# A two-model float32 block on one core: weights of the second half split once, kept in DRAM as two parts

## The chip, the cores and the metric

One core of one Trainium2 chip runs the whole program. The metric is device time in microseconds (us), the median of several runs; the kernel before takes 2792.99 us (2792.43 to 2793.49 in 3 runs). Engines are named TensorE (PE; its weight load PEld), VectorE (DVE), ScalarE (ACT), GpSimd (POOL) and SyncE (SP), which issues most of the DMAs.

## The reference, cut to what matters

Two models are chained over 1024 tokens of width 1024. The first has two layers: a short convolution (layer 1) and dilated attention with 8 heads and three rates (layer 2). The second has one sparse attention layer, in which every query keeps its 256 best keys, and a gated feed-forward with a short convolution.

```
y = short_conv_mixer(h, conv_w_in, conv_w_out)          # w0i, w0o
y = dilated_mixer(h, dil_w_in, dil_w_out, cos, sin)     # w1i, w1v, w1o
...
c_q, c_kv, k_idx, w_idx = split(h @ w_in)               # w2i, w2k
q = (c_q @ w_uq).reshape(B, T, A_HEADS, A_HEAD_DIM)     # w2uq
q_idx = (c_q @ w_qi)                                    # w2q
score = where(key_pos <= q_pos, einsum(wb, relu(q_idx . k_idx)), -inf)
_, sel = lax.top_k(score, n_sel)                        # 256 of up to 1024 keys
return o @ w_o                                          # w2uk, w2uv, w2o
...
u, v = split(h @ w_in, 2); u = conv(u) + conv_b         # w3i, D_FF = 2816
return (gelu(u) * v) @ w_out                            # w3o
```

The comments give the names that the kernel uses for the weights. All is float32.

## The kernel before, in words

Every large product is done as three matmuls: a float32 operand is split into a high part (a copy rounded to the matmul's float32r form) and a low part (the rest), and high x high, high x low and low x high are summed in PSUM (`gemm`, `mm3`). Splitting a weight block of 128 x 1024 costs a ScalarE copy (L338) and a subtraction (L339), on GpSimd unless told otherwise. `weight` (L332 to L340) does this through a ring of three slots, each of a raw, a high and a low buffer of 1024 words:

```
raw, hi, lo = (wring[j][i] for j in range(3))
dma(v(raw.f), src)
A.activation(hi.r[:, :n], raw.f[:, :n], AF.Copy)
(lo_engine or G).tensor_sub(lo.r[:, :n], raw.f[:, :n], hi.f[:, :n])
```

The tokens are worked in two chunks of 512. Layer 1's input and layer 2's input projection use a weight block for both chunks at once (48 matmuls of 512 columns). From layer 2's out-projection on, the chunks are worked at different times, and each weight block is loaded and split again for the second chunk (24 matmuls per load).

The order of the program: layer 1 with its modulation vectors (to about 280 us), its out-projection (`outproj` with w0o, to about 560), layer 2's values, then its 8 heads (`block` and `attend`, to about 1320). A head has seven blocks of w1i, a rotation of queries and keys (`rotate`, L691 to L702, on ScalarE, VectorE and GpSimd), and `attend`, which exchanges small statistics through DRAM (L765 to L774). Then `finish_layer1` (w1o), `project` (w2i, w2k, w2q), `keys` (w2uk, w2uv), and the selection: `topk` finds the 256th best score by a binary search of 31 steps over the bits of a float. Each step counts (L1222 on VectorE for some blocks of queries, L1219 on ScalarE for others) and decides (L1228, L1231, L1242: on one or two numbers per partition, VectorE). The first search runs with `project` and `keys` of the first chunk; the second with the out-projection w2o of the first chunk and the start of its feed-forward. `attention` works the heads (w2uq is split in `head_query`, K and V are loaded on GpSimd's queue), `finish_dsa` is w2o, `ffn_in` is w3i (44 blocks per chunk), `ffn_out` w3o (24 blocks per chunk). The second chunk's attention is interleaved with the first chunk's `ffn_in`.

Each engine works its instructions in a fixed order that is written at build time by a scheduler with a timeline model; buffers of the arena (`ar.new`) are pages that are handed out in the program's order. SP's queue is one such order: a DMA that waits holds back all DMAs behind it.

## Time and profile before

| | |
|---|---|
| median of 3 runs | 2792.99 us |
| profiled execution: time, span | 2787.4 us, 2785.7 us |
| granted TensorE clock, mean (1.0 is 2.4 GHz) | 0.977 |
| TensorE busy | 2609.2 us (94%) |
| VectorE busy | 1588.0 us (57%) |
| ScalarE busy | 1196.7 us (43%) |
| GpSimd busy | 1333.1 us (48%) |
| moved by DMA | 345.18 MB, mean 124 GB/s |

Busy shares are means over stages with different limits, so the table only says that TensorE is the engine to look at. What a stage loses is TensorE's idle time in it, together with time that it spent at the lower clock; what ends that idle time stands in the waits of the stage.

### The profile page before, as it was taken

Reading aid. Unit: us, or ns where it says so; the run is one execution under the profiler, and the core shown is the slowest. Engines: PE = TensorE matmul, PEld = TensorE weight load, DVE = VectorE, ACT = ScalarE, POOL = GpSimd, SP = SyncE. Lnnn points to the kernel's source line nnn. Section 1 sums busy time; section 2 is a strip of 40 time slices with the busy share of each in tenths; the row PEclk is TensorE's granted clock in tenths of the full one; section 3 lists DMA queues with packets and bytes.
Section 4 is the critical chain, followed back from the end, with each engine's and each line's share of the span. In section 5 each row is a group of like instructions: output and inputs, shape, how many; then the busy total and the mean of one; then the engine's idle time right before and its main releaser. Section 6 shows DMA issues by size and latency. Waiting matters only on the chain. (4 is left out here: it accounts for less than half of the span.)

```text
span 2785.7 us, 33753 instructions
## 1 busy us (share of the span) xinstructions
PE 2609.2 (94%) x12070; PEld 2134.6 (77%) x12070; DVE 1588.0 (57%) x3188; ACT 1196.7 (43%) x2032; POOL 1333.1 (48%) x918
## 2 busy tenths in 40 slices
PE   8998999999999999999899778887999989999998
PEld 7876888788888888888777556766787868876787
DVE  7687223204565556556775998997766640434411
ACT  4211224324444544445435667665555543232322
POOL 1122337425645663565475564444544475444453
PEclk9999999999999999999999889999999999999999
DMA  7487224411111111111334534533444643443432
GB/s 289 163 269 242 82 76 165 149 50 56 59 45 64 61 48 52 61 61 55 122 126 151 190 98 141 198 116 113 147 140 134 220 149 106 146 145 133 146 116 72
DMA packets 159141, 345.18 MB, mean 124 GB/s; under 512 B 18386, under 2 KB 58362, under 8 KB 158972
## 3 DMA queue, kind: packets, MB, share of 16 engines
q1 hardware_dynamic: 149612, 317.71, 34.5%
q0 software_dynamic: 9216, 25.17, 3.1%
q8 instruction: 95, 1.56, 0.2%
q14 instruction: 74, 0.61, 0.1%
q10 hardware_dynamic: 144, 0.14, 0.0%
HBM read 285.67 MB, written 58.86 MB: 124 GB/s over the span
## 5 line engine op out<-in xcount | busy, mean ns | idle before, releaser
L254 PE MATMUL p<-page,wring 128*128 128x512 f32 (+2 forms) x8586 | 2022.0, 393 | 80.9 <-DVE page L1476 15.1
L254 PEld LDWEIGHTS p<-page,wring 128*128 128x128 f32 (+1 forms) x8586 | 1598.1, 189 | 440.4 <-POOL wring L339 24.7
L339 POOL TENSOR_TENSOR wring<-wring,wring 128x1024 fp32r<-128x1024 f32 (+1 forms) x283 | 687.8, 2431 | 761.4 <-ACT wring L338 668.3
L254 PE MATMUL p<-page,page 128*128 128x512 f32 (+5 forms) x2816 | 578.6, 350 | 57.4 <-ACT page L345 11.4
L254 PEld LDWEIGHTS p<-page,page 128*128 128x128 f32 (+1 forms) x2816 | 460.3, 196 | 147.4 <-ACT page L814 15.0
L338 ACT ACTIVATE wring<-wring 128x1024 fp32r<-128x1024 f32 (+1 forms) x283 | 293.8, 1040 | 404.4 <-PE p L254 373.1
L346 POOL TENSOR_TENSOR page<-page,page 128x512 fp32r<-128x512 f32 (+2 forms) x111 | 168.2, 1522 | 219.1 <-ACT page L345 209.8
L345 ACT ACTIVATE page<-page 128x512 fp32r<-128x512 f32 (+2 forms) x168 | 110.5, 667 | 306.6 <-DMA page<-d 164.0
L693 POOL TENSOR_TENSOR page<-page,page 128x512 f32<-128x512 f32 x96 | 131.0, 1373 | 128.2 <-ACT page L692 127.8
L299 DVE SCALAR_TENSOR_TENSOR page<-page,page 128x1024 f32<-128x1024 f32 x88 | 117.2, 1332 | 34.2 <-DMA page<-wmod 33.7
L695 DVE TENSOR_TENSOR page<-p,page 128x512 f32<-128x512 f32 x96 | 65.2, 685 | 121.1 <-ACT page L692 104.9
L1496 DVE SCALAR_TENSOR_TENSOR page<-p,page,page 128x512 f32<-128x512 f32 (+1 forms) x17 | 12.2, 719 | 204.2 <-PE p L254 204.2
L346 DVE TENSOR_TENSOR page<-page,page 128x512 fp32r<-128x512 f32 (+1 forms) x57 | 65.2, 1152 | 95.4 <-ACT page L345 90.1
L1469 DVE TENSOR_SCALAR page<-page,page 128x512 f32<-128x512 f32 x44 | 71.7, 1629 | 80.0 <-ACT page L1463 80.0
L702 POOL TENSOR_TENSOR page<-page,page 128x512 fp32r<-128x512 f32 x64 | 97.2, 1519 | 33.3 <-ACT page L701 33.3
L1219 ACT ACTIVATE page<-page,page 128x1024 bf16<-128x1024 f32 (+1 forms) x93 | 86.7, 932 | 60.3 <-DVE page L1242 47.1
L700 DVE TENSOR_TENSOR page<-page 128x512 f32<-128x512 f32 x64 | 82.3, 1295 | 50.0 <-POOL page L693 50.0
L691 ACT ACTIVATE page<-p 64x512 f32<-64x512 f32 x96 | 57.2, 596 | 93.0 <-PE p L254 63.5
L1475 ACT ACTIVATE page<-page 128x512 f32<-128x512 f32 x44 | 27.8, 631 | 141.5 <-DVE page L1473 141.4
L701 ACT ACTIVATE page<-page 128x512 fp32r<-128x512 f32 x64 | 57.0, 890 | 71.7 <-DVE page L700 71.3
L641 DVE SCALAR_TENSOR_TENSOR page<-p,page,page 128x512 f32<-128x512 f32 x48 | 35.8, 746 | 85.0 <-PE p L254 84.0
L1222 DVE TENSOR_SCALAR_CACHE_REDUCE page<-page,page 128x768 bf16<-128x768 f32 (+1 forms) x93 | 81.5, 876 | 1.5
(206 smaller groups left out, 2332.2 us busy)
## 6 DMA issues: line engine op xcount, KB each, us to landing
page<-wmod SPq DMA_DIRECT2D x88, 512.0 KB, 4.3
wring<-w3i SPq DMA_DIRECT2D x88, 512.0 KB, 3.4
d<-page SPq DMA_DIRECT2D x137, 256.0 KB, 2.3
page<-d SPq DMA_DIRECT2D x121, 256.0 KB, 3.2
wring<-w1i SPq DMA_DIRECT2D x56, 512.0 KB, 3.2
d<-page SPq DMA_DIRECT2D x32, 512.0 KB, 4.5
page<-d POOLq DMA_DIRECT2D x32, 512.0 KB, 6.8
wring<-w3o SPq DMA_DIRECT2D x32, 512.0 KB, 3.6
```

The costliest lines, as they stand in the source:

```text
L254: lastn["mm"] = T.matmul(out, lhsT=l, rhs=r, start=start, stop=stop)
L299: V.scalar_tensor_tensor(w.f, w.f, 1.0, sil[j // 6].f, op0=OP.mult, op1=OP.mult, accum_out=m)
L338: A.activation(hi.r[:, :n], raw.f[:, :n], AF.Copy)
L339: (lo_engine or G).tensor_sub(lo.r[:, :n], raw.f[:, :n], hi.f[:, :n])
L345: A.activation(hi.r[:, :n], src, AF.Copy)
L346: (engine or V).tensor_sub(lo.r[:, :n], src, hi.f[:, :n])
L693: G.tensor_mul(sw.f, sw.f, rope[1].f[:, CH(c)])
L700: V.tensor_tensor(a.f, a.f, sw.f, op=OP.add)
L702: G.tensor_sub(out[1], shape(a.f), out[2])
L1219: A.activation(junk.b[:, 0:sc.n], sc.f, AF.Sign, scale=-1.0, bias=at, accum_out=one)
L1222: V.tensor_scalar(junk.b[:, 0:sc.n], sc.f, at, None, op0=OP.is_ge, op1=OP.add, accum_out=one)
L1469: V.tensor_scalar(g.f[:, :512], tv(2), kc(2), col("fb")[:, f:f + 1], op0=OP.mult, op1=OP.add)
```

## The change

A generator `ready` goes over w1o, w2i, w2k, w2q, w2uk, w2uv, w2uq, w2o, w3i and w3o, 102 blocks. For each it loads the block, copies the high part on ScalarE, subtracts on VectorE, and writes both parts to a DRAM tensor. Its steps are taken in the out-projection of layer 1 and in layer 2's heads; what is left is finished behind the last head. `weight` of such a block is then one DMA of both parts (1 MB for a block of 128 x 1024), for either chunk. The ring keeps its nine buffers, as three pairs of high and low and three raw ones; behind layer 2 the raw ones become a fourth pair. `weight_own`, which split one block of w1o into buffers of its own, goes.

```diff
-        wring = []
-        for j in range(3):
-            t = views(sp.tile([128, 1024 * NRING], F32, name=f"wring{j}"))
-            wring.append([Buf(None, None, t, 1024 * i, 1024) for i in range(NRING)])
+        pair = lambda t, i: tuple(Buf(None, None, t, 2048 * i + 1024 * j, 1024) for j in range(2))
+        t = views(sp.tile([128, 2048 * NRING], F32, name="wring"))
+        wring = [pair(t, i) for i in range(NRING)]
+        pairs = [t[0][:, 2048 * i:2048 * i + 2048] for i in range(NRING)]
+        wraw = views(sp.tile([128, 1024 * NRING], F32, name="wraw", tag="wraw"))
+        wraw = [Buf(None, None, wraw, 1024 * i, 1024) for i in range(NRING)]
...
+        def ready(names):
+            for name in names:
+                if name == "w3o":
+                    srcs = {(k, a): I[name][k][:, a:a + m] for k in range(8)
+                            for a, m in ((0, 8), (8, 8), (16, 6))}
...
+                prepared[name] = {}
+                for i, src in srcs.items():
+                    n = math.prod(src.shape[1:])
+                    raw, hi = ar.new(n), ar.new(n)
...
+                    dma(flat, src)
+                    A.activation(hi.r[:, :n], raw.f[:, :n], AF.Copy)
+                    V.tensor_sub(raw.r[:, :n], raw.f[:, :n], hi.f[:, :n])
+                    t = dram([128, 2, n])
+                    dma(t[:, 0], hi.f[:, :n])
+                    dma(t[:, 1], raw.f[:, :n])
+                    prepared[name][i] = Ready(t)
+                    raw.free()
+                    hi.free()
+                    yield
...
         def weight(src, k=8, m=128, lo_engine=None):
-            i = wat[0] % NRING
+            i = wat[0] % len(wring)
...
-            raw, hi, lo = (wring[j][i] for j in range(3))
+            hi, lo = wring[i]
             v = lambda a: a[:, :n].rearrange("p (k m) -> p k m", k=k)
+            if isinstance(src, Ready):
+                dma(pairs[i].rearrange("p (l n) -> p l n", l=2)[:, :, :n], src.t)
+                return v(hi.r), v(lo.r)
+            raw = wraw[i]
...
+        later = Steps(ready(["w1o", "w2i", "w2k", "w2q", "w2uk", "w2uv", "w2uq", "w2o", "w3i", "w3o"]))
...
                     p = block(off + 8 * g + h)
+                    later.go()
...
             p = block(56 + h)
+            later.go(2)
...
             attend(h, q, k, vs, sz)
+            later.go(3)
+        later.finish()
...
+        t = views(sp.tile([128, 1024 * NRING], F32, name="wring2", tag="wraw"))
+        wring.append(pair(t, 0))
+        pairs.append(t[0][:, 0:2048])
...
-                p = gemm(weight(I["w2i"][b]), H2, (c,))[c]
+                p = gemm(weight(prepared["w2i"][b]), H2, (c,))[c]
...
-            raw, w = ar.new(296), new2(296)
-            dma(raw.f[:, 0:256], I["w2uq"][h])
-            split(*w, raw.f[:, 0:256], engine=G)
-            raw.free()
+            w = new2(296)
+            for i in range(2):
+                dma(w[i].f[:, 0:256], prepared["w2uq"][h].t[:, i])
...
-                w = weight(I["w3i"][f])
+                w = weight(prepared["w3i"][f])
```

The line `later.go()` also stands in `each` of layer 1's out-projection. The other uses (w1o, w2k, w2q, w2uk, w2uv, w2o, w3o) are changed like w2i. The lines of the changed kernel lie higher: the ring's subtraction stays in `weight`, L357, L359, L361 and L362 are the load, the subtraction and the two stores of `ready`, and L381 is the ring's load of raw blocks.

The scheduler writes the order of all engines anew. Three places follow, as the order of instructions on an engine; a row has the line, the operation, out<-in by buffer names, and the shape.

GpSimd in the out-projection of the first chunk's sparse attention, with the second search (L402 adds squares, L382 is a power). Before:

```order
L339 TENSOR_TENSOR wring_65<-wring_63,wring_64 128x1024 x3
L402 TENSOR_TENSOR page_11443<-page_11443,page_12721 128x512
L339 TENSOR_TENSOR wring_65<-wring_63,wring_64 128x1024
L402 TENSOR_TENSOR page_11443<-page_11443,page_12755 128x512
L339 TENSOR_TENSOR wring_65<-wring_63,wring_64 128x1024
L402 TENSOR_TENSOR page_11443<-page_11443,page_12789 128x512
L339 TENSOR_TENSOR wring_65<-wring_63,wring_64 128x1024
```

The change (L446 and L426 are the same adds and the power):

```order
L446 TENSOR_TENSOR page_11995<-page_11995,page_13258 128x512
L446 TENSOR_TENSOR page_11995<-page_11995,page_13290 128x512
L446 TENSOR_TENSOR page_11995<-page_11995,page_13322 128x512
L446 TENSOR_TENSOR page_11995<-page_11995,page_13354 128x512
L446 TENSOR_TENSOR page_11995<-page_11995,page_13386 128x512
L446 TENSOR_TENSOR page_11995<-page_11995,page_13418 128x512
L426 TENSOR_TENSOR page_3919<-page_3919,page_65 128x4
```

The weight subtractions between the adds are gone; so it is in all of GpSimd's order behind layer 2.

VectorE in a head of layer 2 (L695 and L698 are steps of the rotation, L346 a split of the values, L933 the gate). Before:

```order
L698 TENSOR_TENSOR page_7432<-page_6735 128x64x8
L346 TENSOR_TENSOR page_7841<-page_7498,page_7840 128x1024
L695 TENSOR_TENSOR page_7626<-p_7775,page_2578 128x512
L698 TENSOR_TENSOR page_7432<-page_7626 128x64x8
L933 SCALAR_TENSOR_TENSOR page_7626<-page_7626,p_7847 128x512
```

The change (L729, L732, L390 and L969 are the same steps):

```order
L359 TENSOR_TENSOR page_7847<-page_7847,page_7854 128x1024
L359 TENSOR_TENSOR page_7862<-page_7862,page_7025 128x1024
L732 TENSOR_TENSOR page_7018<-page_7855 128x64x8
L729 TENSOR_TENSOR page_7826<-p_8237,page_2592 128x512
L732 TENSOR_TENSOR page_7722<-page_7826 128x64x8
L729 TENSOR_TENSOR page_7847<-p_8238,page_2592 128x512
L732 TENSOR_TENSOR page_7722<-page_7847 128x64x8
L390 TENSOR_TENSOR page_8310<-page_7862,page_8309 128x1024
L359 TENSOR_TENSOR page_7847<-page_7847,page_7854 128x1024
L969 SCALAR_TENSOR_TENSOR page_7854<-page_7854,p_8316 128x512
```

Three of a head's nine or ten preparations now stand among these steps.

SP's queue in a head of layer 2 (L863 stores a head's result, L922 loads its values). Before:

```order
L337 DMA wring_63<-w1i 128x1024 x2
L863 DMA d_3151<-page_6648 128x512 x2
L337 DMA wring_63<-w1i 128x1024
L922 DMA page_6544<-d_3153 128x8x128
L337 DMA wring_63<-w1i 128x1024 x2
L922 DMA page_6735<-d_3153 128x1024
```

The change:

```order
L362 DMA d_6490<-page_5375 128x1024
L357 DMA page_6204<-w3i 128x1024
L362 DMA d_6271<-page_5367 128x1024
L357 DMA page_6168<-w3i 128x1024
L361 DMA d_6417<-page_6189 128x1024
L381 DMA wraw<-w1i 128x1024
L362 DMA d_6417<-page_6168 128x1024
L357 DMA page_6189<-w3i 128x1024
L381 DMA wraw<-w1i 128x1024
```

Loads and stores of the preparations now stand between the loads of w1i.

## Rows read from the trace of the kernel before

**Rows 1.** The page's first part: busy us (share of the span) xinstructions.
```profile
PE 2609.2 (94%) x12070; PEld 2134.6 (77%) x12070; DVE 1588.0 (57%) x3188; ACT 1196.7 (43%) x2032; POOL 1333.1 (48%) x918
```

**Rows 2.** Stretches: length, busy PE PEld DVE ACT POOL, clock, DMA share, GB/s.
```profile
696.40:1323.20 626.80, 618.04 (x3148) 520.53 (x3147) 375.90 (x803) 298.15 (x549) 350.14 (x260) 1.00 0.17 56
1323.20:1532.10 208.90, 193.09 (x898) 154.10 (x896) 139.86 (x226) 98.97 (x174) 121.73 (x72) 0.98 0.40 133
1532.10:1741.10 209.00, 161.57 (x722) 124.17 (x722) 195.64 (x581) 142.47 (x326) 112.96 (x130) 0.90 0.47 143
1741.10:1950.00 208.90, 174.69 (x720) 138.18 (x720) 189.36 (x415) 130.55 (x210) 94.68 (x54) 0.94 0.43 142
1950.00:2228.60 278.60, 267.64 (x1315) 222.32 (x1316) 181.18 (x410) 152.95 (x239) 132.24 (x118) 0.98 0.50 161
2228.60:2298.20 69.60, 59.06 (x241) 46.08 (x240) 31.76 (x30) 29.41 (x45) 52.16 (x31) 0.93 0.47 149
2298.20:2785.70 487.50, 465.73 (x2080) 379.65 (x2078) 141.00 (x165) 142.04 (x185) 229.65 (x114) 0.99 0.38 123
```

**Rows 3.** Timeline from 1754 us: start us, us, engine, line, operation, xcount.
```profile
1754.83 20.34 PE L254 MATMUL p<-page,wring 128*128 128x512 f32 x89
1754.90 0.16 DVE L1242 SCALAR_TENSOR_TENSOR page<-page 128x2 int32<-128x2 int32 x1
...
1756.35 4.77 POOL L339 TENSOR_TENSOR wring<-wring,wring 128x1024 fp32r<-128x1024 f32 x2 [9.89 <-ACT wring L338]
1756.50 2.27 DVE L1242 SCALAR_TENSOR_TENSOR page<-page 128x2 int32<-128x2 int32 x1
...
1765.00 0.16 DVE L1228 TENSOR_SCALAR page<-page 128x2 int32<-128x2 f32 x1
```

**Rows 4.** VectorE by form, 1532.1 to 1950.0 us: xcount | busy us, mean ns.
```profile
L1242 DVE SCALAR_TENSOR_TENSOR page<-page 128x2 int32<-128x2 int32 x60 | 23.8, 403 | 0.5
L1222 DVE TENSOR_SCALAR_CACHE_REDUCE page<-page,page 128x512 bf16<-128x512 f32 x31 | 23.1, 744 | 0.6
...
L1242 DVE SCALAR_TENSOR_TENSOR page<-page 128x1 int32<-128x1 int32 x59 | 19.5, 352 | 0.3
L1228 DVE TENSOR_SCALAR page<-page 128x2 int32<-128x2 f32 x32 | 16.9, 528 | 0.2
```

**Rows 5.** Groups of instructions of the whole span, columns as rows 4.
```profile
L339 POOL TENSOR_TENSOR wring<-wring,wring 128x1024 fp32r<-128x1024 f32 (+1 forms) x283 | 687.8, 2431 | 761.4 <-ACT wring L338 668.3
...
L338 ACT ACTIVATE wring<-wring 128x1024 fp32r<-128x1024 f32 (+1 forms) x283 | 293.8, 1040 | 404.4 <-PE p L254 373.1
```

**Rows 6.** Stretches of rows 2, the instructions of L339 alone.
```profile
1532.10:1741.10 209.00, 23.05 (x10) 0.90 0.47 143
1741.10:1950.00 208.90, 66.79 (x27) 0.94 0.43 142
```

**Rows 7.** TensorE's waits, 2228.6 to 2785.7 us: us in total, times, longest.
```profile
PE p L254 <- POOL wring L339: 9.9, 22, 1.7
PE p L254 <- ACT page L345: 4.4, 1, 4.4
PE p L254 <- DVE page L346: 2.6, 1, 2.6
```

**Rows 8.** Groups of instructions of the whole span, columns as rows 4.
```profile
L693 POOL TENSOR_TENSOR page<-page,page 128x512 f32<-128x512 f32 x96 | 131.0, 1373 | 128.2 <-ACT page L692 127.8
...
L510 DVE TENSOR_TENSOR page<-page,page 128x1024 fp32r<-128x1024 f32 x8 | 9.7, 1220 | 0.2 <-ACT page L509 0.2
```

**Rows 9.** Timeline of SP at the start, columns as rows 3.
```profile
13.27 0.33 SPq L298 DMA_DIRECT2D page<-wmod  x1
14.55 0.33 SPq L307 DMA_DIRECT2D page<-wshift  x1
```

**Rows 10.** Timeline of TensorE at the start, columns as rows 3.
```profile
42.25 32.99 PE L254 MATMUL p<-page,page 128*128 128x512 f32 x158 [0.65 <-DVE page L412]
```

**Rows 11.** DMA issues: out<-in, queue, xcount, KB each, median us to landing.
```profile
wring<-w3i SPq DMA_DIRECT2D x88, 512.0 KB, 3.4
```

More of the change, by code (lines that the diff above doesn't have):

```diff
@@ L328, in emit, with __init__ @@
         wat = [0]
+        class Ready:
+            def __init__(self, t):
+                self.t = t
+        def ready(names):
[3 more added lines that the diff above has]
+                            for a, m in ((0, 8), (8, 8), (16, 6))}
+                elif name in ("w2k", "w2q"):
+                    srcs = {0: I[name]}
+                else:
+                    srcs = {i: I[name][i] for i in range(I[name].shape[0])}
+                prepared[name] = {}
+                for i, src in srcs.items():
+                    n = math.prod(src.shape[1:])
+                    raw, hi = ar.new(n), ar.new(n)
+                    flat = raw.f[:, :n]
+                    if len(src.shape) == 3:
+                        flat = flat.rearrange("p (k m) -> p k m", k=src.shape[1])
+                    dma(flat, src)
[8 more added lines that the diff above has]
+                    yield
+        prepared = {}
         def weight(src, k=8, m=128, lo_engine=None):
-            i = wat[0] % NRING
+            i = wat[0] % len(wring)
             wat[0] += 1
             n = k * m
-            raw, hi, lo = (wring[j][i] for j in range(3))
+            hi, lo = wring[i]
             v = lambda a: a[:, :n].rearrange("p (k m) -> p k m", k=k)
+            if isinstance(src, Ready):
+                dma(pairs[i].rearrange("p (l n) -> p l n", l=2)[:, :, :n], src.t)
+                return v(hi.r), v(lo.r)
+            raw = wraw[i]
             dma(v(raw.f), src)
@@ L619, in emit, with outproj @@
                 modvec(pending.pop(0))
-        def weight_own(src, bufs):
-            raw, hi, lo = ar.new(1024), *new2(1024)
-            dma(raw.f.rearrange("p (k m) -> p k m", k=8), src)
-            A.activation(hi.r, raw.f, AF.Copy)
-            G.tensor_sub(lo.r, raw.f, hi.f)
-            raw.free()
-            bufs.extend((hi, lo))
-            return tuple(b.r.rearrange("p (k m) -> p k m", k=8) for b in (hi, lo))
-        def outproj(win, Y, c, gate, xold, xnew, each, apart=()):
-            for k in range(8):
-                mine = []
-                w = weight_own(win[k], mine) if k in apart else weight(win[k])
-                p = gemm(w, Y, (c,))[c]
-                for b in mine:
-                    b.free()
+        later = Steps(ready(["w1o", "w2i", "w2k", "w2q", "w2uk", "w2uv", "w2uq", "w2o", "w3i", "w3o"]))
+        def outproj(win, Y, c, gate, xold, xnew, each):
+            for k in range(8):
+                p = gemm(weight(win[k]), Y, (c,))[c]
                 lastn[3] = lastn["mm"]
@@ L908, in emit @@
                     p = block(off + 8 * g + h)
+                    later.go()
                     for c in range(2):
@@ L974, in each @@
                 xs.append(x)
-            for _ in outproj(I["w1o"], Yc, c, mods[:, 40:48], X1, None, each,
-                             () if c else (3,)):
+            for _ in outproj(prepared["w1o"], Yc, c, mods[:, 40:48], X1, None, each):
                 yield
@@ L1095, in project @@
             normed(0, col("gq"))
-            p = gemm(weight(I["w2k"], 8, 72), H2, (c,), 72)[c]
+            p = gemm(weight(prepared["w2k"][0], 8, 72), H2, (c,), 72)[c]
             kx = ar.new(512)
@@ L1115, in project @@
             free_h(H2, c)
-            whi, wlo = weight(I["w2q"], 2, 512)
+            whi, wlo = weight(prepared["w2q"][0], 2, 512)
             for b in range(4):
@@ L1139, in keys @@
             for i in range(2):
-                whi, wlo = weight(I["w2uk"][i])
+                whi, wlo = weight(prepared["w2uk"][i])
                 for h in range(4):
@@ L1149, in keys @@
             for i in range(2):
-                whi, wlo = weight(I["w2uv"][i], 2, 512)
+                whi, wlo = weight(prepared["w2uv"][i], 2, 512)
                 for t in range(4):
@@ L1434, in each @@
                 xs.append(x)
-            drive(outproj(I["w2o"], Y2, c, mods[:, 64:72], XF, X3, each))
+            drive(outproj(prepared["w2o"], Y2, c, mods[:, 64:72], XF, X3, each))
             free_h(Y2, c)
@@ L1522, in ffn_out @@
                     for a, n in parts:
-                        accumulate(p, weight(I["w3o"][k][:, a:a + n], n), a, n, whole)
+                        accumulate(p, weight(prepared["w3o"][k, a], n), a, n, whole)
                     finish(p, k, x, whole)
                 else:
-                    ws = [(weight(I["w3o"][k][:, a:a + n], n), a, n) for a, n in parts]
+                    ws = [(weight(prepared["w3o"][k, a], n), a, n) for a, n in parts]
                     for w in ws:
```

3 lines of the change are left out of this document (1 added, 2 removed).

## The prediction

> **What bounds the kernel now.** I read the page's busy times first, then the busy time of each engine by stretch, then the waits of the stretches in which TensorE stands still. TensorE is busy for 2609.2 of 2785.7 us [rows 1], so 176.5 us of idle time are all that any change around it can win, beside what the clock gives back. The stretches say where the 176.5 us lie [rows 2]. Layer 2's heads lose 626.80 - 618.04 = 8.8 us of 626.8. The end of layer 2 loses 15.8. The two stretches of the selection (1532 to 1950 us: binary search, first attention, its out-projection, first part of the feed-forward) lose 209.00 - 161.57 = 47.4 and 208.90 - 174.69 = 34.2, together 81.6 us, at granted clocks of 0.90 and 0.94, so some of their busy time ran at the 1.2 GHz level, after the gaps. The second attention loses 11.0, the turn at 2228.6 us 10.5, the feed-forward after it 21.8; the 27.0 left lie ahead of layer 2's heads. So nearly half of the idle time stands in one place, and there VectorE is the engine that is full: 195.64 of 209.00 and 189.36 of 208.90 us.
>
> What fills VectorE there is partly waiting for GpSimd. In the timeline the search's step on two numbers (L1242, 128x2) takes 0.16 us, and 1.6 us later the same step takes 2.27 us; it begins 0.15 us after GpSimd began two weight subtractions (L339) that run for 4.77 us together [rows 3]. By form, L1242 means 403 and 352 ns for 60 and 59 instructions and L1228 528 ns for 32, against 0.16 us in the timeline, while L1222, the long count of the same search, keeps its 744 ns [rows 3, 4]. The excess is 60 x 0.243 + 59 x 0.192 + 32 x 0.368 = 37.7 us of VectorE time in these 418 us, in three rows. The Trainium skill (SBUF — State Buffer, Who interferes with whom) states the same as a rule: an instruction of VectorE with two SBUF inputs contends with one of GpSimd that reads SBUF, the second to issue is blocked until the first ends, and the accumulating tensor_scalar takes no part. The trace agrees, with 2.27 against 0.16 us and the steady 744 ns.
>
> **The change part by part.** *Removed.* Of 283 splits through the ring [rows 5], those of w0i, w0o and w1i (24 + 16 + 56) stay; 187 go, each 1.04 us of ScalarE and 2.43 us of GpSimd: 194 us and 454 us. With them go one split of w1o and 16 of w2uq. What that is worth depends on the stretch.
>
> Selection, 1532 to 1950 us. L339 takes 23.05 and 66.79 us of GpSimd there [rows 6] and all of it goes. The worth is not shown by any row of before, so I bound it. Below nothing: the search is a chain of dependent steps and could be just as long. Above 81.6 us, all the idle time. I take 38 us, the excess worked out above: where VectorE is full and TensorE waits for it, time that VectorE gets back is time that the stretch loses. Other instructions of GpSimd hold some of those 37.7 us too, and will go on doing so; against that, the feed-forward's steps in the same stretch are held up as well and are not in the three rows, and ScalarE gets its splits back. I let these cancel.
>
> Feed-forward and output, 2228.6 to 2785.7 us. TensorE waits 9.9 us for L339 itself, 22 times [rows 7]; each such wait becomes one for a DMA that was issued at least two blocks earlier. I take the 9.9, call it 10. Second attention, 1950.0 to 2228.6: 11.0 us idle; between nothing and that I take 3. End of layer 2: 15.8 us idle, mostly reloading of the heads' results; I take 2. Turn at 2228.6: TensorE waits 4.4 and 2.6 us for splits of reloaded heads (L345, L346) [rows 7] while GpSimd is busy for 52.16 of 69.60 us [rows 2]; without L339 its share of these splits comes sooner; between nothing and 7.0 I take 4.
>
> *Added.* 102 preparations, each one load, one ScalarE copy, one VectorE subtraction, two stores. The nearest row for the subtraction is L510, the same shape, 1.22 us [rows 8]; for the copy 1.04 us [rows 5]. In all 124 us of VectorE and 106 us of ScalarE, moved off the full stretch. By the order given above, 7 of them (w2uq) stand at the very start, 18 before layer 2's heads, one more of w2uq follows, 76 stand within the heads: 9.5 per head, 11.6 us of VectorE.
>
> At the start the 7 add 21 transfers of 128 KB, 2.75 MB, on SP among loads that leave one by one, 512 KB each 1.28 us [rows 9]. All of it in front of TensorE would be 2.75 / 0.524 x 1.28 = 6.7 us; none would be nothing. Only three loads stand ahead of the shift weights that TensorE's first phase still needs, and from 42.25 us TensorE has a run of its own [rows 10], so I take 2 us.
>
> In the heads VectorE is busy for 375.90 of 626.80 us, ScalarE for 298.15 and GpSimd for 350.14 [rows 2]; with 93 and 79 us more they stand at 75% and 60%. Cover is the weight blocks: TensorE has seven blocks per head, each 48 matmuls or 11.0 us (20.34 us for 89 [rows 3]), so a preparation can be late by several us before anyone waits. If that cover fails, every subtraction in front of an attention step costs its 1.22 us. Between nothing and 76 x 1.22 = 93 us I take one per head, 8 x 1.22 = 10 us, nearest to the 8.8 us that are lost now. The w1i loads and a head's small exchanges (L800 to L808) queue on SP behind stores that wait for ScalarE and VectorE; the three slots of the raw ring are 33 us deep, so the loads have time, and the exchanges add to a chain that the same blocks cover. I put no more on them.
>
> The same rule of the Trainium skill speaks against this part. The subtraction has two SBUF inputs, and GpSimd reads SBUF in more than half of this stretch (350.14 of 626.80 us). If each preparation met a multiplication of GpSimd (L693, 1.37 us [rows 8]) halfway, VectorE would lose 76 x 0.56 x 0.69 = 29 us more. By the rule this is spare VectorE time as long as the cover holds, and the sum stays; where it does not hold, it is the third rival's price.
>
> Later, each block of 24 matmuls needs 1 MB in place of 512 KB. By the pace above 24 matmuls take 5.5 us, so 191 GB/s against 410 GB/s that the start shows (0.524 MB in 1.28 us [rows 9]). A load of 512 KB lands in 3.4 us [rows 11]; even twice that, 6.8 us, is under the three blocks that a ring of four leaves it. I cost it at nothing; its cover is the ring. In all five times 49 MB are added to 345 MB.
>
> **Sum.** -38 - 10 - 3 - 2 - 4 + 2 + 10 = -45 us. The profiled execution took 2787.4 us, 5.6 below the median of the runs shown (2792.99), so -45 gives 2742.4 for an execution like it and 2748 us as a median.
>
> **Rivals.** *The chain stays.* The search's rounds are bound by ScalarE's counts and by the exchange of each round, and VectorE's time back turns into idle VectorE. For: the rounds alternate between engines. Against: VectorE idles for only 13.4 and 19.5 us there [rows 2]. Then the 38 fall away: -7, 2786 us, which is at the edge of what can be told from no change; some of the small gains would make it 2780.
>
> *It pays more.* With VectorE free, nearly all 81.6 us close and the clock stays at its upper level. -81.6 - 19 + 2 + 10 = -89, 2704 us. For: the gaps are many and follow VectorE. Against: part of the stretch is attention, whose own chain of steps stays.
>
> *The heads of layer 2 pay (slower).* Preparations stand in VectorE's queue ahead of steps of attention that TensorE waits for, and each is held by GpSimd before it runs: 1.22 + 1.37 = 2.6 us. It decides the sign once more than (57 - 2) / 2.6 = 21 of the 76 lie in TensorE's way. At half of them, 38 x 2.6 = 99 us against the 10 taken: -45 + 89 = +44, 2837 us. Against it: 8.8 us idle in 626.8 today, with 60% of VectorE busy.
>
> *The doubled loads are late.* If the ring did not hide them, each block of 5.5 us would wait for 6.8 us of load: 1.3 us at each of some 150 blocks, +195 us less the gains, near 2940. Against it: the rate at the start. The Trainium skill (DMA: Bandwidth & Descriptors, Bandwidth) gives 6.15 us for 1 MB, also longer than a block; by that, with nothing overlapped, it would be 0.65 us per block, about +98. No run here shows a load of that size.
>
> That the change does less than it says is excluded by the order: no subtraction of weights is left on GpSimd behind layer 2.
>
> **How the numbers follow.** Forecast 0.60, the chain stays 0.15, pays more 0.15, heads pay 0.08, late loads 0.02. What a measurement of this kernel can tell from no change is about 0.2%, 5.6 us. The forecast lies on the faster side with nearly all its chance (0.58), so does paying more (0.15); the chain's case is split, 0.11 faster and 0.04 same. With 0.02 of the forecast's upper tail, same has 0.06; the rest, 0.10, is slower. Faster: 0.84. The range goes from the low end of paying more, 2704, to where the chain stays, 2787; outside it are the two slower cases and the far tails, about 0.2.
>
> **What would show it.** In the profile after: 96 subtractions left on the ring's line of GpSimd and 102 new ones on VectorE at about 1.2 us; L1242's successor near 0.16 to 0.25 us in the mean; 30 to 50 us less idle time of TensorE in the selection; about 10 us more in layer 2's heads; 590 MB moved and no wait of TensorE on a DMA of the ring beyond 2 us. The prediction is wrong if the search's steps are short and TensorE's idle time there is not, if the heads lose over 25 us, or if the blocks of the feed-forward stand apart by more than 5.5 us.

## The result, and the profile after

The changed kernel takes 2908.86 us (median of 4 runs, 2903.88 to 2913.03), against 2792.71 us for the kernel before on the same chip: a ratio of 1.0421 (1.0407 to 1.0434). It is slower by 116 us, where 2748 us was forecast. The profiled execution has a span of 2905.3 us.

The page's first part after, which answers to [rows 1], then stretches in the columns of [rows 2]: the heads in the same window as before, a stretch of the same length as the two selection rows that holds the two searches, and what follows it.

```profile
PE 2653.3 (91%) x12070; PEld 2183.2 (75%) x12070; DVE 1573.2 (54%) x3290; ACT 1113.2 (38%) x1932; POOL 914.3 (31%) x714
```

```profile
696.40:1323.20 626.80, 535.71 (x2513) 444.57 (x2512) 372.23 (x701) 285.48 (x495) 298.73 (x209) 0.92 0.51 177
1679.00:2097.00 418.00, 379.63 (x1705) 303.44 (x1704) 360.44 (x1043) 265.18 (x540) 128.62 (x149) 0.95 0.67 225
2097.00:2390.00 293.00, 287.28 (x1418) 241.62 (x1417) 152.95 (x413) 128.27 (x209) 54.63 (x83) 0.99 0.68 229
2390.00:2905.30 515.30, 494.66 (x2231) 409.24 (x2230) 118.58 (x192) 80.14 (x132) 57.30 (x44) 0.98 0.63 218
```

TensorE's idle time went from 176.5 to 252.0 us and its busy time from 2609.2 to 2653.3 us, with the same 12070 matmuls, at a mean granted clock of 0.951 where it was 0.977. Both stand in the heads. There 8.8 us of 626.8 were idle at a clock of 1.00; now 91.1 us are, at 0.92, and only 2513 of 3148 matmuls were done in the window. The searches are better: 38.4 us idle in 418 us, where [rows 2] had 81.6. These two windows are equal in length and not in work (1705 matmuls against 1442), so here are the searches by their own first and last deciding step (L1242 before, L1282 after):

```profile
1528.80:1920.20 391.40, 315.89 (x1353) 245.42 (x1352) 360.78 (x949) 263.62 (x525) 199.06 (x178) 0.92 0.47 148
1733.80:2064.40 330.60, 292.23 (x1299) 231.96 (x1299) 302.71 (x939) 230.17 (x477) 109.94 (x133) 0.94 0.68 225
```

Their idle time is 75.5 us before and 38.4 after, with 54 matmuls fewer. Behind the searches 5.7 + 20.6 = 26.3 us are idle, where [rows 2] had 43.3.

How long the heads take is read from one matmul per head, the transposition ahead of the small exchange of statistics (L762 before, L796 after). First and last start, by line, before and after:

```profile
L762 PE MATMUL p<-page x4: 271/271/271, 687.0 to 1264.9; 128*16 128x128 f32 x4
L762 PE MATMUL p<-page,page x4: 270/271/271, 880.6 to 1357.9; 128*16 128x128 f32 x4
```

```profile
L796 PE MATMUL p<-page x5: 271/271/271, 701.6 to 1316.1; 128*16 128x128 f32 x5
L796 PE MATMUL p<-page,page x3: 271/271/277, 1198.3 to 1558.2; 128*16 128x128 f32 x3
```

From the first exchange to the eighth are 1357.9 - 687.0 = 670.9 us before and 856.6 us after: 186 us more for seven heads. This interval, **the seven heads**, is the yardstick of the experiments. By these marks and those of the searches, the 119.6 us between the two spans are +14.6 up to the first exchange, +185.7 in the seven heads, +4.7 from there to the searches, -60.8 in the searches and -24.6 behind them.

Who made TensorE, and then ScalarE, wait in the heads after (waits from 690 to 1400 us: us in total, times, longest). The first row is TensorE's largest entry of the kernel before, the next two of the kernel after:

```profile
PE p L254 <- ACT page L814: 9.0, 15, 0.9
...
PE p L257 <- DVE page L729: 41.1, 14, 4.7
PE p L846 <- DVE page L836: 30.7, 8, 7.4
```

```profile
ACT page L725 <- DMA d<-page: 61.1, 24, 8.2
...
ACT page L358 <- DMA page<-w3i: 49.4, 14, 8.4
```

One such wait in the timeline, engine by engine (SP's DMAs, ScalarE, VectorE, TensorE):

```profile
845.32 0.33 SPq L361 DMA_DIRECT2D d<-page  x1
847.10 0.33 SPq L362 DMA_DIRECT2D d<-page  x1
```

```profile
848.74 1.06 ACT L358 ACTIVATE page<-page 128x1024 fp32r<-128x1024 f32 x1 [2.96 <-DMA page<-w3i]
851.36 0.59 ACT L725 ACTIVATE page<-p 64x512 f32<-64x512 f32 x1 [1.57 <-DMA d<-page]
851.97 0.59 ACT L726 ACTIVATE page<-p 64x512 f32<-64x512 f32 x1
```

```profile
852.59 0.69 DVE L729 TENSOR_TENSOR page<-p,page 128x512 f32<-128x512 f32 x1 [0.56 <-ACT page L726]
```

```profile
853.34 2.93 PE L257 MATMUL p<-page,wring 128*128 128x512 f32 x6 [4.17 <-DVE page L729]
```

ScalarE waits 2.96 us for a load of w3i, because the copy L358 is next in its order. Then the rotation (L725) waits 1.57 us more for a store: its scratch buffer lies on a page that a preparation wrote, and the page is free only when the store has landed. The rotation is what empties the PSUM bank that TensorE's next block needs.

A second loss is in TensorE's own order. Timeline of TensorE across the exchange in the second head, before and after:

```profile
784.61 0.27 PE L762 MATMUL p<-page 128*16 128x128 f32 x1
784.63 6.63 PE L254 MATMUL p<-page,wring 128*128 128x512 f32 x28
791.20 0.23 PE L772 MATMUL p<-page,page 16*128 16x16 f32 x1
791.36 3.47 PE L254 MATMUL p<-page,wring 128*128 128x512 f32 x14
```

```profile
822.06 2.99 PE L257 MATMUL p<-page,wring 128*128 128x512 f32 x12
824.89 0.27 PE L796 MATMUL p<-page 128*16 128x128 f32 x1
827.71 0.20 PE L806 MATMUL p<-page,page 16*128 16x16 f32 x1 [2.54 <-DMA page<-d]
832.51 3.29 PE L846 MATMUL p<-page,page 128*128 128x128 f32 x12 [4.59 <-DVE page L836]
```

Before, 28 matmuls of a weight block stood behind the transposition and 14 more behind the second one, 10.1 us of cover for the exchange and the scaling after it. After, none stands there in this head, and 4 to 20 in the next five; TensorE waits for the exchange (2.54 us) and then for the scaling (L836, 4.59 us). The blocks are worked in other places of the order.

### The profile page after: what moved, and what is told of

It is laid out like the page before. It is cut to its first block, busy times and chain, and to the rows that moved or that the text cites. A ratio compares the mean times of both kernels' runs of the same rounds, so it can differ in the third digit from the quotient of the medians.

```text
span 2905.3 us, 34243 instructions
## 1 busy us (share of the span) xinstructions
PE 2653.3 (91%) x12070; PEld 2183.2 (75%) x12070; DVE 1573.2 (54%) x3290; ACT 1113.2 (38%) x1932; POOL 914.3 (31%) x714
## 4 chain that ended last, share of the span: by engine, by line
PE 61%; DMA 15%; DVE 14%; ACT 4%; issue 3%; POOL 2%; SPq 0%; DVEq 0%; POOLq 0%; ACTq 0%
PE p L257 59%; DMA d<-page 7%; DMA page<-wmod 3%; DVE page L302 2%; DMA page<-d 2%; DVE page L359 2%; DMA page<-w3i 1%; ACT page L358 1%; PE p L1414 1%; POOL page L727 1%; PE p L846 1%; DVE page L453 1%; DMA page<-w3o 1%; DVE page L456 1%; DVE page L1230 1%
## 5 line engine op out<-in xcount | busy, mean ns | idle before, releaser
L257 PE MATMUL p<-page,wring 128*128 128x512 f32 (+1 forms) x8610 | 2036.1, 396 | 113.3 <-DVE page L729 47.5
L257 PEld LDWEIGHTS p<-page,wring 128*128 128x128 f32 x8610 | 1628.5, 192 | 471.7 <-DVE page L729 51.5
L257 PE MATMUL p<-page,page 128*128 128x512 f32 (+5 forms) x2786 | 593.2, 358 | 80.8 <-ACT page L389 13.6
L383 POOL TENSOR_TENSOR wring<-wraw,wring 128x1024 fp32r<-128x1024 f32 x96 | 249.8, 2603 | 319.7 <-ACT wring L382 303.9
L390 POOL TENSOR_TENSOR page<-page,page 128x512 fp32r<-128x512 f32 (+1 forms) x95 | 150.2, 1586 | 496.9 <-ACT page L389 480.5
L727 POOL TENSOR_TENSOR page<-page,page 128x512 f32<-128x512 f32 x96 | 151.1, 1579 | 299.8 <-ACT page L726 293.6
L359 DVE TENSOR_TENSOR page<-page,page 128x1024 fp32r<-128x1024 f32 (+3 forms) x98 | 146.1, 1495 | 155.1 <-ACT page L358 154.6
L389 ACT ACTIVATE page<-page 128x512 fp32r<-128x512 f32 (+1 forms) x152 | 104.4, 695 | 286.8 <-DMA page<-d 125.5
L446 POOL TENSOR_TENSOR page<-page,page 128x512 f32<-128x512 f32 x40 | 53.9, 1347 | 293.1 <-ACT page L445 286.7
L358 ACT ACTIVATE page<-page 128x1024 fp32r<-128x1024 f32 (+2 forms) x102 | 100.4, 987 | 115.9 <-DMA page<-w3i 49.4
L382 ACT ACTIVATE wring<-wraw 128x1024 fp32r<-128x1024 f32 x96 | 101.1, 1055 | 97.9 <-PE p L257 89.5
L729 DVE TENSOR_TENSOR page<-p,page 128x512 f32<-128x512 f32 x96 | 65.7, 686 | 110.7 <-ACT page L726 109.2
L725 ACT ACTIVATE page<-p 64x512 f32<-64x512 f32 x96 | 57.1, 595 | 95.0 <-DMA d<-page 70.7
L390 DVE TENSOR_TENSOR page<-page,page 128x512 fp32r<-128x512 f32 (+1 forms) x57 | 56.3, 998 | 68.7 <-ACT page L389 68.5
L1369 POOL TENSOR_TENSOR page<-page,page 128x256 f32<-128x256 f32 x64 | 47.1, 744 | 118.7 <-DVE page L1389 61.4
```

The lines of the kernel that those rows point to most:

```text
L257: lastn["mm"] = T.matmul(out, lhsT=l, rhs=r, start=start, stop=stop)
L359: V.tensor_sub(raw.r[:, :n], raw.f[:, :n], hi.f[:, :n])
L389: A.activation(hi.r[:, :n], src, AF.Copy)
L390: (engine or V).tensor_sub(lo.r[:, :n], src, hi.f[:, :n])
L727: G.tensor_mul(sw.f, sw.f, rope[1].f[:, CH(c)])
```

## The experiments

Each run has the kernel before measured beside it; "against before" is the difference of the two medians of that run.

**Gain alone.** Only the first block of each weight and shape is prepared.

```diff
+ same = [r for r in prepared[name].values() if r.t.shape[2] == math.prod(src.shape[1:])]
+ if same:
+     prepared[name][i] = same[0]
+     continue
```

> Of each weight (and shape) only the first block is prepared, 11 preparations in place of 102; all later blocks load that one pair of parts, so the output uses wrong weights, but every load, matmul and step behind the heads is kept. It gives the gain of the change without its cost. By the traces before and after, the stages behind the heads lost 222 us before and 160 after, so I expect 2793 - 62, about 2730 us (2715 to 2750), if the preparations are the whole of the slowdown. If the doubled loads (1 MB per block) or the new order of the stages cost something of their own, it stays above 2793.

Measured: 2708.75 us, ratio 0.9687 (0.9666 to 0.9708), 88 us faster than before; seven heads 669.4 us. TensorE: 2591.7 us busy in a span of 2705.6, so 113.9 us idle. The gain is real and larger than the 2715 to 2750 us that were expected; the two searches, the second attention and the rest are these stretches of this kernel:

```profile
1532.10:1950.00 417.90, 371.55 (x1685) 295.99 (x1684) 366.76 (x1096) 265.87 (x530) 132.75 (x163) 0.95 0.65 217
1950.00:2180.00 230.00, 227.06 (x1114) 190.29 (x1114) 115.26 (x300) 90.57 (x157) 35.35 (x55) 0.99 0.68 228
2180.00:2705.60 525.60, 506.02 (x2272) 418.57 (x2270) 118.78 (x192) 80.91 (x133) 60.63 (x47) 0.98 0.65 220
```

The doubled loads are all in it (of one pair of parts per weight and shape), and they cost nothing that shows. All the loss of the change, 116 + 88 = 204 us, belongs to the other 91 preparations.

**Without stores; DMA alone.** The first computes each preparation and stores only the first of each weight; the second loads each block twice (into both pages) and stores both, without copy and subtraction.

```diff
+ if same:
+     prepared[name][i] = same[0]
+ else:
      t = dram([128, 2, n])
```

```diff
- A.activation(hi.r[:, :n], raw.f[:, :n], AF.Copy)
- V.tensor_sub(raw.r[:, :n], raw.f[:, :n], hi.f[:, :n])
+ if any(r.t.shape[2] == n for r in prepared[name].values()):
+     dma(hi.f[:, :n]..., src)
+ else:
+     A.activation(hi.r[:, :n], raw.f[:, :n], AF.Copy)
+     V.tensor_sub(raw.r[:, :n], raw.f[:, :n], hi.f[:, :n])
```

> All 102 blocks are loaded, copied on ScalarE and subtracted on VectorE, but only the first of each weight is stored (wrong weights later, as in the first experiment). Theory of pages: a preparation keeps two arena pages until its stores have landed, and SP's queue waits on them; the scratch buffers of the rotation wait for these pages, and TensorE behind them. Then, without stores, most of the 187 us that the heads and layer 1's out-projection lose go, and the time falls to 2740 to 2790 us. Theory of engines: the copy and the subtraction stand in the in-order queues of ScalarE and VectorE ahead of steps that TensorE waits for. Then the cost stays and the time is 2850 or more.

> The other half: for all blocks but the first of each weight the copy and the subtraction are left out; the block is loaded into both pages and both are stored (so the weights behind it are raw, not split: wrong output, and one load of 512 KB more per block than the changed kernel). Theory of pages: still slow, 2870 us or more. Theory of engines: no instruction of ScalarE or VectorE is left of a preparation, so the time falls to 2730 to 2770 us.

Measured: 2841.56 us without stores (45 above before; seven heads 784.5), 2868.94 us with DMA alone (72 above; 818.6). Neither theory holds alone: over the run of the gain the two cost 133 and 160 of the 204 us. They are not two halves, for both hold the loads, and the second has one load per block more than the change, so its 160 may overstate the DMA part. Without stores the second to seventh heads keep the cover of the exchange, 28 to 40 weight-block matmuls at the places of the change; timeline of the fourth head:

```profile
1041.96 0.27 PE L800 MATMUL p<-page 128*16 128x128 f32 x1
1041.98 9.36 PE L257 MATMUL p<-page,wring 128*128 128x512 f32 x40
1051.27 0.23 PE L810 MATMUL p<-page,page 16*128 16x16 f32 x1
```

**Subtraction on GpSimd.**

```diff
- V.tensor_sub(raw.r[:, :n], raw.f[:, :n], hi.f[:, :n])
+ G.tensor_sub(raw.r[:, :n], raw.f[:, :n], hi.f[:, :n])
```

> The subtraction of the preparations is put on GpSimd in place of VectorE, nothing else. If VectorE's queue is what delays the steps, TensorE's waits for VectorE's rotation step (47.5 us after) shrink and the time falls to 2800 to 2850 us. If it is the pages, a subtraction of 2.4 us in place of 1.2 us holds them longer: 2900 us or more.

Measured: 2910.02 us (113 above before; seven heads 858.5). The time is that of the change. This does not clear VectorE, for the order differs as well: no weight-block matmul stands behind the transposition in the second to seventh heads, where the change has 0 to 20. It also says that the time does not follow the count of these matmuls alone.

**Compute alone, and its halves.** From w2uq on, 79 preparations keep copy and subtraction at their places, on resident data, without load and store; then only the copies; then only the subtractions.

```diff
+ if same and name in ("w2uq", "w2o", "w3i", "w3o"):
+     A.activation(hi.r[:, :n], rope[0].f[:, :n], AF.Copy)
+     V.tensor_sub(raw.r[:, :n], rope[0].f[:, :n], hi.f[:, :n])
+     prepared[name][i] = same[0]
...
```

> From w2uq on, all blocks but the first of each weight keep the copy and the subtraction, at the same places, but read a tensor that is resident in the heads (the rotation's cosines) and are not stored: no load and no store of a preparation is left there, 79 of 102 (later blocks load the first one's parts: wrong weights). The stores cost at most 68 us (2910 - 2842), and the whole preparation 201 over the run that has 11 of them (2709). If the waiting is for DMA (a copy on ScalarE that waits for its load, a page that waits for its store), this run falls to within 25 us of that one, 2709 to 2735. If the engines' own work in their queues costs, 79 x (1.04 + 1.22) = 179 us bounds it, and I would see 2760 or more.

> As the run without loads and stores in the heads (2777 us), but without the 79 subtractions on VectorE: of a preparation there only the copy on ScalarE is left. If ScalarE's copies in front of the rotation and the attention's steps are the engine cost, it stays near 2777 (2765 to 2785). If VectorE's subtractions are, it falls to 2710 to 2730.

> The other half: only the 79 subtractions on VectorE are left there, of two resident tensors, and no copy on ScalarE. If VectorE is the engine cost: near 2777 (2760 to 2785); if ScalarE is: 2710 to 2730. If both add up, this and the copies alone lie between, near 2740 to 2750 each.

Measured, against before: -20 us for both (2776.74), -67 for the copies (2723.42), -28 for the subtractions (2762.37). Seven heads: 726.4, 678.0 and 711.5 us, against 669.4 with neither. So ScalarE's copies by themselves cost 9 us there, VectorE's subtractions 42, both together 57 (72 or 73 of them stand in the seven heads, where the change has 76 preparations). In the run of the subtractions, 65 full ones mean 1445 ns (by form, from 626 to 1420 us):

```profile
L356 DVE TENSOR_TENSOR page<-page,page 128x1024 fp32r<-128x1024 f32 x65 | 93.6, 1445 | 4.3 <-DMA d<-page 2.1 <-POOL page L744 1.2 <-PE p L257 0.6
```

These runs keep the cover of the exchange: 28 to 37 weight-block matmuls stand behind the transposition in the second to seventh heads with compute alone or subtractions alone, at the places of the change. Compute alone misses the 2709 to 2735 that were expected of waiting for DMA alone; with the DMAs, 116 + 20 = 136 us more are lost. At the places of the change the seven heads thus go from 669.4 to 726.4 us with compute, to 784.5 with the loads too and to 856.6 with the stores: 57 + 58 + 72 = 187 us.

**Loads a step ahead, and its control.** In the first, a step issues one load and finishes the block of the step before; pages are given back a step later; the two steps between gate block and attention move behind the attention. The control makes that move alone. Both take one step less per head than the change, so that 68 or 69 of their subtractions stand in the seven heads and 10 behind them, where the change has 76 and 1.

```diff
  dma(flat, src)
- A.activation(hi.r[:, :n], raw.f[:, :n], AF.Copy)
- V.tensor_sub(raw.r[:, :n], raw.f[:, :n], hi.f[:, :n])
...
+ if made:
+     finish_one()
+ made.append((name, i, n, raw))
```

```diff
  p = block(56 + h)
- later.go(2)
...
  attend(h, q, k, vs, sz)
- later.go(3)
+ later.go(4)
```

> Everything is computed as in the changed kernel. A step now issues the load of one block, and copies, subtracts and stores the block loaded a step before; the pages of a block are given back another step later, and all are given back ahead of the value loads of a head; the two steps behind the gate block move behind the attention. If ScalarE's wait for loads and the rotation's wait for stores are what costs, both shrink (ScalarE waited 69 us for loads of w3i and w3o and 71 us in front of L725): 2800 us or less. If the cost is the number of pages taken from a full arena, or the DMA traffic itself, nothing is won: 2880 to 2930.

> Control for the run with loads a step ahead (2821 us), which had also moved the two steps behind the gate block: here only that move is made, one to four steps behind the attention, and the load stays in front of its own copy. If the load ahead and the later release of pages did it, this stays at 2890 or more; if the place did it, it falls to about 2830.

Measured: 2821.13 us with loads ahead (25 above before; seven heads 738.1), but 2843.66 us with the move alone (54 above; 759.5). So the move gives 116.2 - 53.6 = 63 us (97 in the seven heads, of which 34 come back elsewhere, most of them behind), and the load ahead with later release only 29 more. With loads ahead neither of the two expected cases came: 2821 us lies between them. My reading that ScalarE's wait for loads was the main cost falls. With the move, the order has its cover back (28 to 37 matmuls in the second to seventh heads); timeline of TensorE in the fourth head of the control:

```profile
1029.67 0.27 PE L796 MATMUL p<-page,page 128*16 128x128 f32 x1
1029.69 6.63 PE L257 MATMUL p<-page,wring 128*128 128x512 f32 x28
1036.26 0.23 PE L806 MATMUL p<-page,page 16*128 16x16 f32 x1
1036.42 3.52 PE L257 MATMUL p<-page,wring 128*128 128x512 f32 x14
```

What stays is the rotation: waits of TensorE and ScalarE, 690 to 1400 us, of the control.

```profile
PE p L257 <- DVE page L729: 48.7, 12, 6.6
```

```profile
ACT page L358 <- DMA page<-w3i: 34.4, 23, 3.8
ACT page L725 <- DMA d<-page: 26.8, 18, 5.1
```

**Ahead of the heads.** Two preparations per step of layer 1's out-projection and two per step of the values, the rest in the heads (the diff); then, with one per step of the out-projection, only the 34 blocks up to w2o, all ahead of the heads, with w3i and w3o split in the ring.

```diff
- later.go()
+ later.go(2)
...
  mm3(p, tok, w, k == 0, k == 7)
+ later.go(2)
  x = ar.new(512)
```

> Two preparations per step of layer 1's out-projection and two in each of the 16 steps of layer 2's values, so 64 of 102 stand ahead of the heads, where the arena has 12 to 15 empty pages in place of 9 or fewer, and 38 stay in the heads in place of 86. If the cost comes per preparation in the heads (184 us / 86 = 2.1 us each), it falls by 48 x 2.1 = 103 us to about 2810, if the values' stage hides its own. If the traffic costs wherever it stands (1.5 MB per preparation), it stays at 2880 or more.

> Only the 34 blocks up to w2o are prepared, one per step of layer 1's out-projection and two per step of the values, none in the heads; w3i and w3o are split in the ring on GpSimd as before, which keeps its three raw buffers. The heads should be as before (about 30 us lost from 627 us on, not 200). The gain behind the heads is then only a part of the 88 us that the first experiment gave: if w3i's splits beside the second search are most of it (67 of the 90 us of splits in 1532 to 1950 us stood there), 2760 to 2790; if it is the first search's, 2720 to 2750.

Measured: 2997.00 us (201 above before) and 2848.72 us (52 above). Both lie above all that was expected: standing where the arena has more empty pages does not help. TensorE's and ScalarE's waits in the first of them, 490 to 770 us (L919 copies the values' PSUM bank):

```profile
PE p L257 <- ACT page L919: 93.2, 7, 23.6
PE p L257 <- ACT page L389: 50.1, 1, 50.1
```

```profile
ACT page L358 <- DMA page<-w3i: 123.9, 24, 7.8
ACT page L919 <- DMA d<-page: 24.0, 8, 4.1
```

Here ScalarE's order is the likely cause: copies that wait for loads stand ahead of the copy that frees TensorE's bank. What held L389, a single wait of 50.1 us, was not followed up. In the second run, which leaves the seven heads as they were (669.6 us), TensorE is idle for 220.0 - 146.3 = 73.7 us from 480 to 700 us, ahead of the heads, against 220.0 - 216.8 = 3.2 us before; that is more than its 52 us, so behind it about 70.5 - 52 = 18 are won.

**Versions that could be better.** No preparations: the first chunk splits in the ring as before and stores both parts from the ring, the second chunk loads them. Then the same with 40, and with 60 blocks prepared, loads a step ahead.

```diff
+ if keep:
+     t = dram([128, 2, n])
+     dma(t, pairs[i].rearrange("p (l n) -> p l n", l=2)[:, :, :n])
+     prepared[keep[0]][keep[1]] = Ready(t)
```

> No preparations at all. The first chunk loads and splits every block in the ring as before; the two parts are stored from the ring to DRAM (1 MB per block, 94 blocks), and the second chunk loads them. w2uq stays as before. This takes only the second chunk's splits off GpSimd, and adds no instruction of ScalarE, VectorE or GpSimd. The second search still stands beside splits of w2o and w3i of the first chunk. If the 88 us of the first experiment come evenly from splits in both chunks, half, about 2750 us (2740 to 2770); if they come mainly from the splits beside the second search, 2775 to 2795. Above 2800 if a ring slot that waits for its store to land (about 5 us) holds up the blocks, 5.5 us apart, behind it.

> As the ring-store run, but the 34 blocks up to w2o and 6 of w3i are prepared early, each load one step ahead of its copy: 24 in layer 1's out-projection of the first chunk, 8 in the second half of the values, one per head behind the attention. Theory: a preparation costs because ScalarE, in order, waits at its copy for a load (52 us for w2o in the run with 34 preparations, 171 us for w3i in the one with 64 ahead of the heads), with TensorE behind it; a load issued a step ahead takes most of that away. Then the stages ahead of the heads lose at most 30 us more than before, and the time is 2740 to 2780. If the loads are still late, 2800 or more.

> As the last, with 26 blocks of w3i prepared (those that stand beside the second search), four preparations per head, all behind the attention of a head and none between its rotations. Against the last run it takes 20 more splits from beside the second search, worth up to 40 us, and adds 28 preparations to the heads; at the 0.7 us that one costs there by its compute alone (54 us for 79) plus some for DMA, 30 to 60 us. So about even with the last: 2740 to 2800.

Measured: 2769.78 us with the ring alone, ratio 0.9910 (0.9888 to 0.9932); 2773.78 us with 40 prepared, 0.9926 (0.9901 to 0.9952); 2818.53 us with 60, 1.0078 (1.0056 to 1.0101). The first two beat both kernels, by 26 and 22 us against before, under 1% but clear of 1.0; the last is above the 2740 to 2800 expected of it. The ring alone adds no instruction of ScalarE, VectorE or GpSimd; 190 subtractions stay on GpSimd in place of 283, and its stores and loads take as long as the change's loads:

```profile
L400 POOL TENSOR_TENSOR wring<-wraw,wring 128x1024 fp32r<-128x1024 f32 (+1 forms) x190 | 466.2, 2455 | 549.0 <-ACT wring L399 443.4
```

```profile
d<-wring SPq DMA_DIRECT2D x85, 1024.0 KB, 5.3
wring<-d SPq DMA_DIRECT2D x85, 1024.0 KB, 5.3
```

With 40 prepared, seven preparations stand in the seven heads, one per head behind the attention, and cost nothing there: 665.4 us against 670.2 with the ring alone. The 32 ahead of the first exchange cost 28 us (719.5 against 691.1 us to its start), about what the 40 bring. With 60, 28 stand in the seven heads, four per head, and these take 733.1 us: 68 more for 21 more preparations. The 62 us to the run of the gain are still to be had; beyond one preparation per head, no place tried costs less than the preparations bring.

## Why the prediction was wrong

**Selection, -38: right.** Idle time of TensorE fell from 81.6 to 38.4 us in windows of equal length (46.4 with the gain alone), and from 75.5 to 38.4 us between the searches' own first and last step. The mechanism is there too; by form, 1679 to 2097 us of the changed kernel:

```profile
L1262 DVE TENSOR_SCALAR_CACHE_REDUCE page<-page,page 128x512 bf16<-128x512 f32 x31 | 23.1, 744 | 0.7
...
L1282 DVE SCALAR_TENSOR_TENSOR page<-page 128x2 int32<-128x2 int32 x60 | 12.7, 226 | 0.5
L1282 DVE SCALAR_TENSOR_TENSOR page<-page 128x1 int32<-128x1 int32 x60 | 10.6, 206 | 0.1
...
L1268 DVE TENSOR_SCALAR page<-page 128x2 int32<-128x2 f32 x32 | 6.1, 192 | 0.0
```

The means were 403, 352 and 528 ns [rows 4]: 60 x 0.177 + 59 x 0.146 + 32 x 0.336 = 30.0 of the 37.7 us came back. Its cause was read rightly: with the weight subtractions gone, the short steps are short, and the accumulating count (L1262, L1222 before) keeps its 744 ns. The run of the ring alone is the control: there the splits of the first chunk still stand beside the second search, 59.96 us of GpSimd from 1740 to 1950 us where it had been 66.79, and the steps of that search stay long:

```profile
L1308 DVE SCALAR_TENSOR_TENSOR page<-page 128x2 int32<-128x2 int32 x60 | 21.5, 366 | 0.5
```

Beside the first search (1500 to 1740 us) GpSimd's weight subtractions fell from 32.77 to 15.25 us, and the steps of that search from 352 ns [rows 4] to 208. For the steps of L1282, which read two SBUF tensors, this agrees with the rule of the Trainium skill (SBUF — State Buffer, Who interferes with whom) that an instruction of VectorE with two SBUF inputs contends with one of GpSimd that reads SBUF. The step of L1268 reads one tensor, which that rule does not name, and went from 528 to 192 ns as well. That VectorE's 30.0 us became 37 us of TensorE's idle time one for one is not shown; the prediction let the other effects cancel.

**Feed-forward, second attention and turn, -10 - 3 - 4 = -17: right.** 43.3 us idle became 26.3 (2.9 + 19.6 = 22.5 with the gain alone, in stretches with fewer matmuls). What I left out is the clock: from the kernel before to the run of the gain, TensorE's idle time fell by 176.5 - 113.9 = 62.6 us, near the 57 forecast for the removal, and its busy time by 17.5 us besides, at a mean granted clock of 0.980 against 0.977.

**Doubled loads at nothing: right.** TensorE waited for the ring once for 1.9 us between 1650 and 2440 us, and for none behind 2440. 1 MB lands in 5.3 us, less than the 6.8 us allowed. The Trainium skill (DMA: Bandwidth & Descriptors, Bandwidth) gives 6.15 us, longer than a block of 5.5 us, for transfers that GpSimd issues; the measured 5.3 us of SP's loads, from issue to landing, decides.

**The heads, +10: this step failed.** It was "one per head, 8 x 1.22 = 10 us", resting on "cover is the weight blocks", with the queue of SP and the exchanges priced at nothing. Measured: 187 us over the seven heads against the run of the gain. The runs take it apart in two ways, which overlap and are not to be added.

By what a preparation does, at the places of the change:

- VectorE's subtractions cost 42 us in the seven heads, 57 with the copies, where 10 was taken and 93 was the upper bound. The subtraction means 1545 ns for 67 from 626 to 1532 us, not 1.22 us, so each is 0.3 us longer, near the 0.56 x 0.69 = 0.4 us that the prediction worked out and took for spare time.
- The loads cost 58 us more and the stores another 72. No term of the sum had either: a copy that waits for its load holds back the rotation behind it on ScalarE, and each preparation keeps two pages until its stores land (4.2 us for 512 KB, in the median), pages that the rotation's buffer waits for.

By where it stands: the cover was taken as given. The prediction rested it on the 11 us of each weight block, and did not ask where the new order would put the blocks. Moving two steps per head behind the attention takes the seven heads from 856.6 to 759.5 us, 97 us, and the whole by 63. That it is this move is shown; that it works through the cover is argued. For it: TensorE's waits at the exchange and the scaling, 34.1 + 3.0 = 37 us in the seven heads of the change, are gone from the control; they are 37 of the 58 us of idle time that the move took away there, and the other 39 of the 97 us are busy time, at a granted clock of 0.95 in place of 0.90. Why the order puts the blocks elsewhere stays open. It does so in the runs with loads and stores at these places, and in none of the runs without stores. Of the places of the order shown ahead of the prediction none is TensorE's in the heads.

**At the start, +2** is not told apart from no change, and around layer 1's out-projection, where no loss was forecast, the first exchange comes 14.6 us later than before: TensorE waits once for 13.6 us for a copy of a split (L389, from 480 to 600 us), where the longest wait before was 3.1 us; what held that copy was not followed up.

**The rivals.** "The heads pay" gave the sign and the place, at a chance of 0.08 and 2837 us; its mechanism, steps of attention behind preparations in VectorE's queue, is a quarter of it. "It pays more", 2704 us, is near what the removal alone gives (2709), but by luck: of the 81.6 us that were to close 46.4 stay, at a clock of 0.95, and the rest of the gain is idle time elsewhere and clock. The chances were wrong because neither loads, pages nor TensorE's order had a price, and because 8.8 us of idle time was taken for slack.

## What to carry to other kernels

That an engine is seldom idle in a stage does not tell how much filler the stage can take: here one preparation per head, behind the attention with its load a step ahead, was free, and nine or ten at the places of the change cost 187 us. Find what covers the stage's waits, and where the new order puts that cover: look at TensorE's order across each small exchange before and after. Work that is put in as filler also holds buffers until its DMAs land, and a copy that waits for its load holds back all that stands behind it on its engine; price both. Where values are made anyway, as in the ring, storing them there gave part of the gain (26 of 88 us) for no instruction of a compute engine.

## What the runs showed that was not expected

The transfers of a filler cost more than its compute: in the seven heads 149 us with DMA alone (818.6 - 669.4, with one load too many per block), 57 with compute alone, and 187 with both. A subtraction of 2.4 us on GpSimd in place of 1.5 us on VectorE left the time as it was (2910 us). And of the 204 us only part is idle time: TensorE's busy time in the changed kernel is 61.6 us above that of the run of the gain (2653.3 and 2591.7), for the same matmuls, and the granted clock in the heads' window, in which TensorE now idles for 91.1 us, is 0.92 in the mean where it was 1.00 with 8.8 us idle.
